# Four of the 22 channel blocks of an up-projection as seven products of halves

## The chip, the cores and the metric

The kernel runs on one core of one Trainium2 chip. The metric is the device time of one execution in microseconds (us). The engines are named as in the profile: PE is the matrix engine, PEld its weight loads, DVE the vector engine, ACT the scalar engine, POOL the third elementwise engine, SP the engine that issues most of the DMA transfers.

## The reference, cut to what matters

The reference is one layer of an encoder on 512 tokens of 1024 channels in float32: a norm, an input projection, two token mixers, a merge, and then a channel mixer. The change touches only the channel mixer:

```
h  = rmsnorm(x)                             # 512 x 1024
u  = h @ w_up                               # 512 x 5632: 2816 gate columns, then 2816 value columns
u  = depthwise conv of width 3 along tokens, centred, with a bias
y  = silu(u[:, :2816]) * u[:, 2816:]        # 512 x 2816
x  = x + y @ w_down                         # 512 x 1024
```

The 2816 channels are 22 blocks of 128. A block needs a gate product and a value product, each of 128 channels by 512 tokens over 1024 inputs.

## The kernel before

Every float32 factor is split into a high and a low part, both in the matrix engine's own float format, and a product is the sum of three: high by high, high by low, low by high. `mm3` issues those three matmuls (L390, L391, L392).

A planner (class `Planner`, L38) collects tasks with an engine, an estimated cost, a key, the names that they read and write, and rings of buffers. It lists them in order of time under its own costs, and the result is one fixed order of instructions for each engine. The engines then run their own orders, and wait on each other through counting semaphores that the framework sets wherever two instructions touch the same tile. A low key means early: FEED (weights) before EVICT (emptying PSUM) before CHAIN (L300).

One up-projection product is one job (`up_job`, L1877; `job`, L433). `weights` (L400) loads 128 columns of `w_up` (512 KB, tile `wr_up`, ring "raw" of three buffers), ACT casts the high half (L413, tile `wh_up`, ring "whi" of two), and POOL subtracts for the low half in two instructions of 128x512 (L421, tile `wl_up`, ring "wlo" of two). Then come 24 matmuls of 128x512 (eight groups of 128 inputs, three each) into one PSUM bank `ps_up` of ring "pp", which has three banks. The token side is `h2` in two parts, shared by all 44 jobs. The first three jobs work on halves of 256 tokens, since `h2` gets ready late.

The bank is emptied by `conv3` (L1943): ACT writes the centre tap with the bias into a tile `c3` (L1948), DVE adds the two outer taps from PSUM (L1954). After a gate and its value, ACT takes the silu (L1976), DVE multiplies (L1974) into `a_0` or `a_1` (blocks 0 to 10 and 11 to 21), and `combine` (L1917) and `split_part` (ACT L1904, DVE L1908) make operands for the down-projection, which already works by seven products of halves (ORDER, TO, L1894). Its weights are prepared in `t_unit` (L1923): two loads of `w_down` rows, four subtractions on POOL (L1939, tile `tp`, ring "tp" of one) and four stores to a scratch tensor; one such unit runs with every second block.

Two other rings matter below: "oo", one tile of two PSUM banks that no job of the up-projection uses, and "dhl", three buffers of 512 KB.

Of the kernel before, what the change touches and what calls it, by code (L numbers as in the profile page):

```python
# [14 lines left out]
P = 128  # L15
S = 512
# [212 lines left out]
def hybrid_block(  # L229
# [1693 lines left out]
    def t_unit(i, u):  # L1923

        b = {}

        def load(r):
            if "w" not in b:
                b["w"] = pools["fp"].tile([P, 2, D], F32, tag="tp", bufs=RINGS["tp"], name=f"tp_{i}")
            k = i + HK * r  # L1930
            sp.dma_start(b["w"][:, r, :], ffn_down[0][k * P : (k + 1) * P, :])

        w = lambda r, c: b["w"][:, r, N_H[c]]
        n = lambda r, c: f"tp:{i}#{r}{c}"
        for r in range(2):
            L(512, lambda r=r: load(r), r=["pool:fp"], w=[n(r, 0), n(r, 1)], key=u, after=() if i else ["pp:up0_1"])

        for j, o, x, y in ((0, (0, 0), (0, 1), (0, 0)), (2, (0, 1), (1, 1), (0, 1)), (1, (1, 1), (1, 1), (0, 0)), (3, (1, 0), (1, 0), (1, 1))):
            G(cp(512), lambda o=o, x=x, y=y: pool.tensor_tensor(out=w(*o), in0=w(*x), in1=w(*y), op=ALU.subtract),  # L1939
              r=[n(*x), n(*y)], w=[n(*o)], key=u)  # L1940
            L(256, lambda j=j, o=o: sp.dma_start(t_scr[j, i], w(*o)), r=[n(*o)], w=[f"ts{j}#{i}"], key=u)

    def conv3(box, pp, ci, b, j, u):  # L1943
        yn = f"cv3:{ci}"

        def centre():
            b[j] = pools["fp"].tile([P, S], F32, tag="cv3", bufs=RINGS["cv3"], name=f"c3_{ci}")
            act.activation(b[j], box["ps"], AF.Identity, scale=fw[:, 1, ci : ci + 1], bias=fw[:, 3, ci : ci + 1])  # L1948

        def tap(k):  # L1950
# [5 lines left out]
                in1=y[:, lo:hi], op0=ALU.mult, op1=ALU.add,  # L1956
            )

        A(0.8, centre, r=[pp, "pool:fp", "small"], w=[yn], key=EVICT + u)
        for k in (0, 2):  # L1960
            V(0.78, lambda k=k: tap(k), r=[pp], w=[yn], key=EVICT + u)

    for c in range(NF):
        b = {}
        for j in range(2):
            box, pp, u = first_jobs.get((c, j)) or up_job(c, j)
            conv3(box, pp, j * NF + c, b, j, u)
        g_, v_ = f"cv3:{c}", f"cv3:{NF + c}"

        def mul(c=c, b=b):  # L1970
            r, i = divmod(c, HK)
            if i == 0:
                a_raw[r] = pools["fp"].tile([P, HK, S], F32, name=f"a_{r}")
            dve.tensor_tensor(out=a_raw[r][:, i, :], in0=b[0], in1=b[1], op=ALU.mult)  # L1974

        A(ca(512), lambda b=b: act.activation(b[0], b[0], AF.Silu), w=[g_], key=u, tab="silu")  # L1976
        V(cd(512), mul, r=[g_, v_], w=[f"ar{c}#0", f"ar{c}#1"], key=u)
        if c < HK:
            split_part(1, c, 1, *blk(c, 0), u + 1)
            s3 = lambda b=b: b[1].rearrange("p (k c) -> p k c", k=2)[:, 0:1]  # L1980
            combine(s3, [v_], blk(c, 0)[0], blk(c, 1)[0], [f"ar{c}"], ALU.subtract, u + 2)
            split_part(7, c, 1, s3, [v_], u + 3)
        else:
            i = c - HK
            combine(*blk(i, 1), blk(i, 1)[0], blk(c, 1)[0], [f"ar{c}#1"], ALU.add, u + 1)
            combine(*blk(i, 0), blk(i, 1)[0], blk(i, 0)[0], [f"ar{i}#1"], ALU.subtract, u + 2)
        if c % 2 == 0:
            t_unit(c // 2, u + 60)


    KEEP = 8
# [248 lines left out]
```

## Time and profile before

| | |
|---|---|
| median of three runs | 874.38 us (873.37 to 874.95) |
| profiled execution, its own time | 874.77 us |
| its span | 873.1 us |
| granted TensorE clock | 0.998 |
| PE busy | 865.3 us, 99% of the span |
| DVE, POOL, ACT busy | 595.0, 532.4, 475.6 us |
| first and last matmul of the up-projection | 518.2 and 760.3 us after the span's start |

The span is the time from the first to the last recorded instruction; the 1.7 us between span and time lie around it. A row of the timeline gives start, duration, engine, line, operation, output and inputs, shapes, and in brackets how long the engine sat idle before it and what ended that. Matmuls are pipelined: the spacing of their starts is their cost, and the duration of one (0.39 us for 128x512) overlaps the next ones.

### The profile page before, as it was taken

What the parts mean: (1) busy time and instruction counts of PE and PEld (TensorE: products, weight loads), DVE (VectorE), ACT (ScalarE), POOL (GpSimd) and SP (SyncE); (2) the same over time, 40 slices, a digit from 0 to 9 for tenths busy, and PEclk for the clock granted to TensorE, in tenths of its full rate; (3) what the DMA queues carried; (4) which work ended last, traced back from release to release, by engine and by line L of the source; (5) the groups of instructions that cost most, each with busy time, mean ns of one, the idle gap of its engine ahead of it and who ended that gap; (6) DMA issues with size and microseconds to landing.
All of it is one profiled execution on the core that took longest, in us unless ns stands there. A gap on an engine that the chain in (4) does not pass through costs nothing.

```text
span 873.1 us, 13883 instructions
## 1 busy us (share of the span) xinstructions
PE 865.3 (99%) x5049; PEld 731.6 (84%) x5049; DVE 595.0 (68%) x1035; ACT 475.6 (54%) x807; POOL 532.4 (61%) x461
## 2 busy tenths in 40 slices
PE   9999999999999999999999999999999999999997
PEld 8888888888888887889888889888888888888886
DVE  5756597357569886555676984656654555579996
ACT  6688554336858634345866665444443333555664
POOL 4445554324546655244597994778777887567763
PEclk9999999999999999999999999999999999999999
DMA  7365447304245463224898005666567666365554
GB/s 210 99 206 134 122 122 165 113 26 133 74 119 157 124 149 93 68 73 134 306 315 281 1 26 155 218 205 209 199 212 237 216 199 198 134 209 181 183 170 151
DMA packets 165512, 138.09 MB, mean 158 GB/s; under 512 B 23662, under 2 KB 133051, under 8 KB 165444
## 3 DMA queue, kind: packets, MB, share of 16 engines
q1 hardware_dynamic: 160706, 135.62, 50.5%
q10 hardware_dynamic: 4738, 1.58, 0.8%
q8 instruction: 40, 0.66, 0.3%
q14 instruction: 28, 0.23, 0.1%
HBM read 113.03 MB, written 24.15 MB: 157 GB/s over the span
## 4 chain that ended last, share of the span: by engine, by line
PE 87%; DVE 6%; POOL 3%; issue 2%; ACT 1%; DMA 1%; POOLq 0%; SPq 0%; DVEq 0%; ACTq 0%
PE ps_up L392 9%; PE ps_up L391 9%; PE ps_up L390 9%; DVE as L1908 2%; PE ps_k L390 2%; PE ps_gd L390 2%; PE ps_k L392 2%; PE ps_gp L390 2%; PE ps_k L391 2%; PE pw L1192 2%; PE ps_gp L392 2%; PE ps_q L392 2%; PE ps_gp L391 2%; PE ps_q L390 2%; PE ps_q L391 2%
## 5 line engine op out<-in xcount | busy, mean ns | idle before, releaser
L421 POOL TENSOR_TENSOR wl_up<-wr_up,wh_up 128x512 fp32r<-128x512 f32 x86 | 111.9, 1322 | 51.8 <-ACT wh_up L413 51.7
L390 PE MATMUL ps_up<-h_hi,wh_up 128*128 128x512 f32 (+1 forms) x360 | 136.8, 380 | 0.0
L392 PE MATMUL ps_up<-h_hi,wl_up 128*128 128x512 f32 (+1 forms) x360 | 136.7, 380 | 0.1
L391 PE MATMUL ps_up<-h_lo,wh_up 128*128 128x512 f32 (+1 forms) x360 | 136.7, 380 | 0.0
L1954 DVE SCALAR_TENSOR_TENSOR c<-ps_up,fw,c 128x511 f32<-128x511 f32 x88 | 66.0, 750 | 99.2 <-ACT c L1948 97.5
L2142 POOL TENSOR_TENSOR w_dn<-wr_dn,w_dn 128x512 fp32r<-128x512 f32 x44 | 65.9, 1513 | 30.9 <-ACT w_dn L2139 27.1
L390 PEld LDWEIGHTS ps_up<-h_hi,wh_up 128*128 128x128 f32 x360 | 67.7, 188 | 12.9
L391 PEld LDWEIGHTS ps_up<-h_lo,wh_up 128*128 128x128 f32 x360 | 67.7, 188 | 12.9
L392 PEld LDWEIGHTS ps_up<-h_hi,wl_up 128*128 128x128 f32 x360 | 67.7, 188 | 12.9 <-POOL wl_up L421 0.3
L413 ACT CAST wh_up<-wr_up 128x1024 fp32r<-128x1024 f32 x43 | 45.2, 1052 | 58.1 <-issue 26.0
L1939 POOL TENSOR_TENSOR tp<-tp 128x512 f32<-128x512 f32 x44 | 61.7, 1402 | 11.7 <-DMA tp<-in_ffn_down_dram 8.0
L2139 ACT CAST w_dn<-wr_dn 128x512 fp32r<-128x512 f32 x69 | 42.2, 621 | 28.6 <-PE dn L392 17.1
L391 PE MATMUL dn<-w_dn,as 128*128 128x512 f32 x141 | 54.3, 385 | 0.0
L390 PE MATMUL dn<-w_dn,as 128*128 128x512 f32 x141 | 54.2, 385 | 0.0
L392 PE MATMUL dn<-w_dn,as 128*128 128x512 f32 x141 | 54.2, 385 | 0.0
L1908 DVE TENSOR_TENSOR as<-a,as 128x512 fp32r<-128x512 f32 (+1 forms) x41 | 41.3, 1032 | 0.1
L1904 ACT CAST as<-a 128x512 fp32r<-128x512 f32 (+1 forms) x41 | 21.5, 535 | 35.0 <-DVE a L1974 30.1
L421 POOL TENSOR_TENSOR wl_k<-wr_k,wh_k 128x512 fp32r<-128x512 f32 x16 | 20.3, 1288 | 28.6 <-ACT wh_k L413 25.6
L1948 ACT ACTIVATE c<-ps_up,fw 128x512 f32<-128x512 f32 x44 | 33.9, 769 | 4.9 <-PE ps_up L392 4.9
L421 POOL TENSOR_TENSOR wl_gp<-wr_gp,wh_gp 128x512 fp32r<-128x512 f32 x16 | 22.3, 1417 | 22.2 <-ACT wh_gp L413 22.2
L421 POOL TENSOR_TENSOR wl_v<-wr_v,wh_v 128x512 fp32r<-128x512 f32 x16 | 21.2, 1347 | 22.7 <-ACT wh_v L413 22.7
L421 POOL TENSOR_TENSOR wl_z<-wr_z,wh_z 128x512 fp32r<-128x512 f32 x16 | 20.4, 1295 | 19.8 <-ACT wh_z L413 19.8
(410 smaller groups left out, 2538.0 us busy)
## 6 DMA issues: line engine op xcount, KB each, us to landing
wr_up<-in_ffn_up_dram SPq DMA_DIRECT2D x44, 512.0 KB, 3.9
tp<-in_ffn_down_dram SPq DMA_DIRECT2D x22, 512.0 KB, 5.2
t_scr<-tp SPq DMA_DIRECT2D x44, 256.0 KB, 2.9
wr_dn<-t_scr SPq DMA_DIRECT2D x20, 512.0 KB, 4.0
wr_dn<-in_ffn_down_dram SPq DMA_DIRECT2D x15, 512.0 KB, 3.7
x<-in_x_dram SPq DMA_DIRECT2D x8, 512.0 KB, 6.4
wr_k<-in_w_in_dram SPq DMA_DIRECT2D x8, 512.0 KB, 4.8
wr_z<-in_w_in_dram SPq DMA_DIRECT2D x8, 512.0 KB, 3.9
```

Of the source, the lines that this page charges most:

```text
L390: pe.matmul(ps, ahi, bhi, start=first, stop=False)
L391: pe.matmul(ps, ahi, blo, start=False, stop=False)
L392: pe.matmul(ps, alo, bhi, start=False, stop=last)
L413: act.copy(b["hi"], b["raw"])
L421: pool.tensor_tensor(out=b["lo"][:, sl], in0=b["raw"][:, sl], in1=f32(b["hi"][:, sl]), op=ALU.subtract)
L1904: act.copy(sets[p][:, i : i + n, 0, :], src())
L1908: dve.tensor_tensor(out=w[:, :, 1, :], in0=src(), in1=f32(w[:, :, 0, :]), op=ALU.subtract)
L1939: G(cp(512), lambda o=o, x=x, y=y: pool.tensor_tensor(out=w(*o), in0=w(*x), in1=w(*y), op=ALU.subtract), r=[n(*x), n(*y)], w=[n(*o)], key=u)
L1948: act.activation(b[j], box["ps"], AF.Identity, scale=fw[:, 1, ci : ci + 1], bias=fw[:, 3, ci : ci + 1])
L1954: dve.scalar_tensor_tensor(out=y[:, lo:hi], in0=box["ps"][:, lo + sh : hi + sh], scalar=fw[:, k, ci : ci + 1], in1=y[:, lo:hi], op0=ALU.mu ...
L2139: act.copy(b["w"][:, 0, :], raw["t"][:, j, :])
L2142: eng.tensor_tensor(out=b["w"][:, 1, :], in0=raw["t"][:, j, :], in1=f32(b["w"][:, 0, :]), op=ALU.subtract)
```

## The change

For channel blocks 4, 6, 8 and 10, `seven_job` takes the place of the gate job and the value job. The 2x2 matrix of weight halves (gate and value rows by first and second 512 inputs) times the 2x2 matrix of token halves (first and second 512 inputs by first and second 256 tokens) is computed as seven products of sums of halves. One product has four input groups of three matmuls of 128x256: 84 such matmuls in place of 48 of 128x512.

- All seven products of a block go into one tile of two PSUM banks, `ps_w` (ring "oo"), with gate in one bank and value in the other, and a half of the tokens in each half of a bank. Product 1 goes to value/first half, 2 to gate/first, 6 to value/first again, 5 to gate/second, 7 to value/second, 4 to value/first, 3 to gate/second.
- Between the products, partial results move: `keep(0)` copies product 1 out to SBUF and `keep(1)` copies a later sum (both ACT, 128x256, L2145). `add_first` adds the first kept piece to both banks in place (DVE, 2x256, L2154), `add_mid` adds the second kept piece to both second halves into an SBUF tile (L2157), `add_end` and `add_last` add those back into PSUM (L2163, L2160). Then `conv3` works on the two banks as before.
- Weights: each block has three sums on POOL and one on DVE (L1986, 128x512), seven casts of 128x512 on ACT (L2081), and seven subtractions for the low parts, four on POOL and three on DVE (L2086), instead of two casts of 128x1024 and four POOL subtractions.
- Tokens: `token_forms`, once, makes four sums of token halves in two parts: 12 instructions of 128x1024 on DVE (nine) and POOL (three) and four casts on ACT. Its buffers are `a_0` for work, one buffer of ring "as", and the place of `a_1`, so the first product into `a_1` (block 11) waits until they are read.
- Moved: one `combine` and the split for product 7 of the down-projection go from blocks 0 to 10 to blocks 11 to 21. The 11 `t_unit`s run with blocks 0, 2, 5, 8, 11 and 12 to 17 instead of every second block, and units 5, 7 and 9 use two "dhl" buffers instead of "tp".

The first place where the order changes is PE at the start of block 6. In the names, `ps_up6_0` is the gate's bank of block 6, `ps_w6` the new two-bank tile, `w_up6f2` the weights of its product 2. Before:

```order
L390 MATMUL ps_up5_1_5905<-h2_hi_5201,wh_up5_1_5864 128x512
L391 MATMUL ps_up5_1_5905<-h2_lo_5202,wh_up5_1_5864 128x512
L392 MATMUL ps_up5_1_5905<-h2_hi_5201,wl_up5_1_5865 128x512
L390 MATMUL ps_up6_0_5945<-h2_hi_5201,wh_up6_0_5909 128x512 [waits DVE_49,Activation_49]
L391 MATMUL ps_up6_0_5945<-h2_lo_5202,wh_up6_0_5909 128x512
L392 MATMUL ps_up6_0_5945<-h2_hi_5201,wl_up6_0_5910 128x512 [waits Pool_49]
```

Each job waits when it starts, for the bank and the two weight parts, and its other matmuls follow. Now, from the last matmul of product 1 on:

```order
L392 MATMUL ps_w6_6002<-h2_hi_5201,w_up6f1_5958 128x256
L390 MATMUL ps_w6_6002<-h2_hi_5201,w_up6f2_5963 128x256 [waits Activation_49]
L391 MATMUL ps_w6_6002<-h2_lo_5202,w_up6f2_5963 128x256
L392 MATMUL ps_w6_6002<-h2_hi_5201,w_up6f2_5963 128x256 [waits DVE_49]
L390 MATMUL ps_w6_6002<-h2_hi_5201,w_up6f2_5963 128x256 [waits Activation_49]
L391 MATMUL ps_w6_6002<-h2_lo_5202,w_up6f2_5963 128x256
```

Product 2 goes to a different bank than product 1, and yet its fourth matmul waits for ACT: the count that it waits for is the one that `keep(0)` raises. The same stands in all four blocks (in block 4 `keep(0)` stands three matmuls later). In the same way, the fourth matmul of product 5 waits for `add_first`, the first of product 7 for `keep(1)`, the seventh of product 4 for `add_mid`, and the first of product 3 for `add_end`. Before the first of product 3 stand three matmuls of 128x512 of the next block's gate; nothing stands between the others and what they wait for. No matmul of the kernel before waits for an access to the tile that it is itself in the middle of filling.

The second place is ACT around the two copies of block 6 (`c3_6` is the block's gate tile, `wh_up7_0` the next gate's high weights, `c3_27` the value tile of block 5):

```order
L2081 CAST w_up6f4_6016<-wr_up6_1_5877 128x512 [waits PE_49]
L2145 COPY c3_6_6025<-ps_w6_6002 128x256 [waits PE_49]
L1962 ACTIVATE c3_27_6031<-ps_up5_1_5953,fw_128 128x512
L2200 ACTIVATE c3_5_5980<-c3_5_5980 128x512 [waits DVE_49,Activation_49]
L413 CAST wh_up7_0_6050<-wr_up7_0_5934 128x1024 [waits DMAHW1_49]
L2145 COPY c3_6_6025<-ps_w6_6002 128x256 [waits DVE_49,PE_49]
```

The first copy waits for PE, and the count is that of product 2's third matmul, not of product 1's last. The second copy waits for DVE (`add_first`) and for PE (the last matmul of product 5).

The third place is DVE, in the same block (`c3_28` is the value tile of block 6, `as_1` an operand of the down-projection):

```order
L1968 SCALAR_TENSOR_TENSOR c3_27_6031<-ps_up5_1_5953,fw_128,c3_27_6031 128x511 [waits DVE_49]
L2154 TENSOR_TENSOR ps_w6_6002<-ps_w6_6002,c3_6_6025 128x2x256 [waits PE_49]
L2198 TENSOR_TENSOR a_0_5498<-c3_5_5980,c3_27_6031 128x512 [waits DVE_49,Activation_49]
L1913 TENSOR_TENSOR as_1_5672<-a_0_5498,as_1_5672 128x256 [waits Activation_49]
L2157 TENSOR_TENSOR c3_28_6102<-ps_w6_6002,c3_6_6025 128x512 [waits PE_49]
L2163 TENSOR_TENSOR ps_w6_6002<-ps_w6_6002,c3_28_6102 128x256 [waits DVE_49,PE_49]
L2160 TENSOR_TENSOR ps_w6_6002<-ps_w6_6002,c3_28_6102 128x2x256 [waits DVE_49,PE_49]
L1968 SCALAR_TENSOR_TENSOR c3_6_6025<-ps_w6_6002,fw_128,c3_6_6025 128x511 [waits DVE_49,Activation_49]
```

`add_first` waits for the third matmul of product 5, `add_mid` for the sixth of product 4, `add_end` for the twelfth of product 4, `add_last` for the end of product 3. Between two of them stand the product and the split of block 5.

The diff, cut to its core:

```diff
+    SEVEN = (4, 6, 8, 10)
+    FORMS = (1, 2, 6, 5, 7, 4, 3)
+    LO_ENG = dict(zip(FORMS, "GVGVGVG"))
+    SUM_ENG = "GVGG"
+    TOK_ENG = "VGVVVVVGVVGV"
...
+    def seven_job(c, b):
...
+        for j in range(2):
+            L(512, lambda j=j: load(j), w=[f"{rn[j]}#0", f"{rn[j]}#1"], key=feed + j)
...
+        total(s1, a21, a22, ALU.add, 2)
+        total(s2, s1, a11, ALU.subtract, 3)
+        for k, (f, src) in enumerate(((1, a11), (2, a12), (6, s2), (5, s1))):
+            wn[f] = form(f, src, k)
+        total(a21, a11, a21, ALU.subtract, 14)
+        total(a12, a12, s2, ALU.subtract, 15)
+        for k, (f, src) in enumerate(((7, a21), (4, a22), (3, a12))):
+            wn[f] = form(f, src, k + 4)
...
+        where = {1: (1, 0), 2: (0, 0), 6: (1, 0), 5: (0, 1), 7: (1, 1), 4: (1, 0), 3: (0, 1)}
...
+        def spot(a, i):
+            if "t" not in ps:
+                ps["t"] = banks2(f"ps_w{c}")
+            return ps["t"][:, a, 256 * i : 256 * i + 256]
...
+        def mm(f, k):
+            w = wt_[f]
+            sl = slice(k * P, (k + 1) * P)
+            mm3(spot(*where[f]), w[:, 0, sl], w[:, 1, sl], *right(f, k), k == 0, k == 3)
...
+        def product(f):
+            for k in range(4):
+                M(0.361, lambda k=k: mm(f, k), r=[wn[f], *rname(f, k)], w=[on(*where[f]), f"turn{c}"], key=u + 10 * turn["n"] + k)
+            turn["n"] += 1
...
+        def keep(i):
+            A(ca(256), lambda: act.copy(pieces(0)[:, i, :], spot(1, 0)), r=[on(1, 0), "pool:fp"], w=[pn[i]], key=top)
...
+        def add_first():
+            dve.tensor_tensor(out=both(0), in0=both(0), in1=twice(pieces(0)[:, 0:1, :]), op=ALU.add)
+
+        def add_mid():
+            dve.tensor_tensor(out=pieces(1), in0=both(1), in1=twice(pieces(0)[:, 1:2, :]), op=ALU.add)
+
+        def add_last():
+            dve.tensor_tensor(out=both(1), in0=both(1), in1=twice(pieces(1)[:, 0:1, :]), op=ALU.add)
+
+        def add_end():
+            dve.tensor_tensor(out=spot(1, 0), in0=spot(1, 0), in1=pieces(1)[:, 1, :], op=ALU.add)
+
+        product(1)
+        keep(0)
+        product(2)
+        product(6)
+        V(cd(512), add_first, r=[pn[0]], w=[on(0, 0), on(1, 0)], key=top)
+        keep(1)
+        product(5)
+        product(7)
+        V(cd(512), add_mid, r=[on(0, 1), on(1, 1), pn[1], "pool:fp"], w=[pn[2], pn[3]], key=top)
+        product(4)
+        product(3)
+        V(cd(512), add_last, r=[pn[2]], w=[on(0, 1), on(1, 1)], key=top)
+        V(cd(256), add_end, r=[pn[3]], w=[on(1, 0)], key=top)
...
+    APART = (5, 7, 9)
+    UNITS = (0, 2, 5, 8, 11, 12, 13, 14, 15, 16, 17)
```

More of the change, by code (lines that the diff above doesn't have):

```diff
@@ L1899, in hybrid_block, with a_half @@
     sets = {}
+    def a_half(r):
+        if a_raw[r] is None:
+            a_raw[r] = pools["fp"].tile([P, HK, S], F32, tag=f"a{r}", name=f"a_{r}")
+        return a_raw[r]
     def part_hi(p, i, n, src):
@@ L1925, in t_unit @@
         b = {}
+        apart = i in APART
         def load(r):
-            if "w" not in b:
-                b["w"] = pools["fp"].tile([P, 2, D], F32, tag="tp", bufs=RINGS["tp"], name=f"tp_{i}")
+            if apart:
+                b[r] = pools["fp"].tile([P, D], F32, tag="dhl", bufs=RINGS["dhl"], name=f"tp_{i}{r}")
+            elif not r:
+                t = pools["fp"].tile([P, 2, D], F32, tag="tp", bufs=RINGS["tp"], name=f"tp_{i}")
+                b[0], b[1] = t[:, 0, :], t[:, 1, :]
             k = i + HK * r
-            sp.dma_start(b["w"][:, r, :], ffn_down[0][k * P : (k + 1) * P, :])
-        w = lambda r, c: b["w"][:, r, N_H[c]]
-        n = lambda r, c: f"tp:{i}#{r}{c}"
+            sp.dma_start(b[r], ffn_down[0][k * P : (k + 1) * P, :])
+        w = lambda r, c: b[r][:, N_H[c]]
+        n = lambda r, c: f"dhl:t{i}{r}#{c}" if apart else f"tp:{i}#{r}{c}"
         for r in range(2):
@@ L1941, in t_unit, with conv3 @@
             L(256, lambda j=j, o=o: sp.dma_start(t_scr[j, i], w(*o)), r=[n(*o)], w=[f"ts{j}#{i}"], key=u)
-    def conv3(box, pp, ci, b, j, u):
+    def conv3(box, pp, ci, b, j, u, late=None):
         yn = f"cv3:{ci}"
+        pp = pp if late else [pp]
         def centre():
-            b[j] = pools["fp"].tile([P, S], F32, tag="cv3", bufs=RINGS["cv3"], name=f"c3_{ci}")
+            if late:
+                box["ps"] = late()
+            if j not in b:
+                b[j] = pools["fp"].tile([P, S], F32, tag="cv3", bufs=RINGS["cv3"], name=f"c3_{ci}")
             act.activation(b[j], box["ps"], AF.Identity, scale=fw[:, 1, ci : ci + 1], bias=fw[:, 3, ci : ci + 1])
@@ L1957, in tap @@
             )
-        A(0.8, centre, r=[pp, "pool:fp", "small"], w=[yn], key=EVICT + u)
+        A(0.8, centre, r=[*pp, "pool:fp", "small"], w=[yn], key=EVICT + u)
         for k in (0, 2):
-            V(0.78, lambda k=k: tap(k), r=[pp], w=[yn], key=EVICT + u)
+            V(0.78, lambda k=k: tap(k), r=pp, w=[yn], key=EVICT + u)
+    SEVEN = (4, 6, 8, 10)
[3 more added lines that the diff above has]
+    TOK_ENG = "VGVVVVVGVVGV"
+    forms = {}
@@ L1963, in hybrid_block @@
+    APART = (5, 7, 9)
+    UNITS = (0, 2, 5, 8, 11, 12, 13, 14, 15, 16, 17)
     for c in range(NF):
         b = {}
-        for j in range(2):
+        if not c:
+            token_forms()
+        if c in SEVEN:
+            u = seven_job(c, b)
+        for j in range(2 if c not in SEVEN else 0):
             box, pp, u = first_jobs.get((c, j)) or up_job(c, j)
```

127 lines of the change are left out of this document (118 added, 9 removed).

## The prediction

> **What bounds the kernel now.** The page's busy times come first, then the chain that ended last, then busy time by stretches of the up-projection.
>
> ```profile
> span 873.1 us, 13883 instructions
> PE 865.3 (99%) x5049; PEld 731.6 (84%) x5049; DVE 595.0 (68%) x1035; ACT 475.6 (54%) x807; POOL 532.4 (61%) x461
> ...
> PE 87%; DVE 6%; POOL 3%; issue 2%; ACT 1%; DMA 1%; POOLq 0%; SPq 0%; DVEq 0%; ACTq 0%
> ```
>
> ```profile
> core 0: us, PE busy (x) PEld busy (x) DVE busy (x) ACT busy (x) POOL busy (x), PEclk, DMA share, GB/s
> 530.00:568.00 38.00, 38.00 (x200) 32.75 (x199) 21.38 (x28) 18.47 (x26) 24.60 (x19) 1.00 0.53 175
> 560.00:600.00 40.00, 40.00 (x178) 33.14 (x177) 21.50 (x29) 18.11 (x26) 30.77 (x24) 1.00 0.67 214
> 600.00:640.00 40.00, 40.00 (x179) 33.10 (x178) 24.87 (x31) 17.57 (x26) 31.30 (x24) 1.00 0.67 224
> 640.00:680.00 40.00, 40.00 (x178) 33.14 (x177) 22.20 (x27) 15.72 (x21) 31.37 (x25) 1.00 0.64 204
> 720.00:765.00 45.00, 45.00 (x200) 37.28 (x199) 25.69 (x33) 19.56 (x28) 29.10 (x23) 1.00 0.50 166
> ```
>
> In every stretch PE is busy for all of it, at full granted clock. So a microsecond of matmul taken out is a microsecond gained, and a microsecond in which PE stands still is one lost, since there is no idle time of PE to absorb it. POOL comes next (31 of 40), then DVE and ACT at about half.
>
> **What is removed: matmul time.** The spacing of the starts tells it. First and last row of two dense stretches of the timeline:
>
> ```profile
> 546.37 0.39 PE L390 MATMUL ps_up<-h_hi,wh_up 128*128 128x512 f32 x1
> ...
> 551.80 0.39 PE L390 MATMUL ps_up<-h_hi,wh_up 128*128 128x512 f32 x1
> ```
>
> ```profile
> 531.74 0.28 PE L390 MATMUL ps_up<-h_hi,wh_up 128*128 128x256 f32 x1
> ...
> 537.50 0.40 PE L390 MATMUL ps_up<-h_hi,wh_up 128*128 128x512 f32 x1
> ```
>
> 24 matmuls of 128x512 lie between the first pair: 5.43/24 = 0.226 us each. 48 of 128x256 lie between the second: 5.76/48 = 0.120. A block cost 48 x 0.226 = 10.86 and will cost 84 x 0.120 = 10.08 of matmul time. That is 0.78 less, and 3.1 us for four blocks: an eighth of 10.86 would be 1.36, and the rest of it goes into the fixed part of the shorter matmuls.
>
> The Trainium skill ("TensorE: Matmul & The Clock Gate", "Back-to-back issue gap") gives N/2.4 + 2.5 ns for an isolated matmul at full clock, so by estimate 215.8 and 109.2 ns, and 1.19 us less for a block, 4.7 in all. The rows have 226 and 120, a fixed part of 14 ns, and they decide; by the page the sum below would end 1.6 us earlier.
>
> **What is added: waits in the middle of a block.** A job of the kernel before waits when it starts, for a bank that was emptied long ago. In the changed order PE waits five times inside a block for an ACT or DVE instruction on the tile that it is filling, and each of these in turn waits for the very matmul before (product 3, below, apart). ACT and DVE cannot come early, so PE pays for the whole way there and back. No row before has such a round trip whole, but its pieces are there:
>
> ```profile
> 531.62 0.28 PE L392 MATMUL ps_up<-h_hi,wlo_up 128*128 128x256 f32 x1
> 532.07 0.78 ACT L1948 ACTIVATE c<-ps_up,fw 128x512 f32<-128x512 f32 x1 [4.88 <-PE ps_up L392]
> 532.88 0.75 DVE L1954 SCALAR_TENSOR_TENSOR c<-ps_up,fw,c 128x511 f32<-128x511 f32 x1 [4.97 <-ACT c L1948]
> ...
> 866.45 0.28 PE L392 MATMUL dn<-wt_lo,as 128*128 128x256 f32 x1
> 866.77 0.42 DVE L2018 TENSOR_TENSOR x<-dn,x 128x256 f32<-128x256 f32 x1 [0.56 <-PE dn L392]
> ```
>
> ```profile
> 521.22 0.28 PE L391 MATMUL ps_up<-h_lo,wh_up 128*128 128x256 f32 x1
> 521.56 0.19 PEld L392 LDWEIGHTS ps_up<-h_hi,wl_up 128*128 128x128 f32 x1 [0.27 <-POOL wl_up L421]
> 521.56 0.39 PE L392 MATMUL ps_up<-h_hi,wl_up 128*128 128x256 f32 x1
> 521.78 0.28 PE L390 MATMUL ps_up<-h_hi,wh_up 128*128 128x256 f32 x1
> ```
>
> ```profile
> L1593 ACT CAST ms<-ps_do x8: 348/372/374, 443.5 to 483.4; 128x256 fp32r<-128x256 f32 x8
> ...
> L1580 DVE TENSOR_TENSOR ps_do<-ps_do,gdl x8: 686/700/700, 441.8 to 477.9; 128x512 f32<-128x512 f32 x8
> ```
>
> - From the start of a matmul of 128x256 to the start of a reader that stood waiting for it: 0.45 (531.62 to 532.07), 0.32 (866.45 to 866.77). Behind the second PE ran dry, as it will here, so I take 0.35.
> - From the end of one engine's instruction to the start of the other that waits: 532.07 + 0.78 = 532.85 to 532.88, 0.03.
> - After a stall the next spacing is 0.22 (521.56 to 521.78), not 0.12: the weight load lies open, 0.10 more. If the weights can be loaded before the wait, it is 0.
> - The access: an ACT copy of 128x256 out of PSUM 0.37, an in-place DVE addition of 128x512 in PSUM 0.70.
>
> A `keep` costs PE 0.35 + 0.37 + 0.03 + 0.10, less the 0.12 that the spacing takes anyway: 0.73 (0.60 with nothing for the weights and 0.32 ahead, 0.83 with 0.45). `add_first` and `add_mid` cost 0.33 more each: 1.06 (0.93 to 1.16). `add_end` (128x256, 0.42 as at 866.77) takes 0.35 + 0.42 + 0.03 = 0.80, and PE has three matmuls of the next gate for it, 0.12 + 3 x 0.226 = 0.80: 0 (to 0.20). `add_last` has nobody on PE waiting for some 10 us. One block: 2 x 0.73 + 2 x 1.06 = 3.58 (3.06 to 4.18); four: 14.3 (12.2 to 16.7).
>
> Whether the waiting engine is free when its matmul is done: ahead of `keep(0)` stands the cast for product 4, which waits for the end of the previous job, 15 matmuls (1.8 us) earlier, and takes some 0.6. Between the two copies stand a centre tap (0.78), a silu and a cast of 128x1024, some 2.5 us together, and PE needs about 5 between them. Ahead of `add_first` stand two taps (0.75 each) that end 2.3 us after `keep(0)`, where PE needs over 3 for the rest of product 2, product 6 and three matmuls. So 0, with 0.5 per block (2 in all) as the upper end. Behind `keep(0)` on ACT are the centre tap of the block before and the cast of the next gate's weights; both are used a product or more later.
>
> **What is added on POOL, DVE and ACT.** Durations, from the groups of the page:
>
> ```profile
> L421 POOL TENSOR_TENSOR wl_up<-wr_up,wh_up 128x512 fp32r<-128x512 f32 x86 | 111.9, 1322 | 51.8 <-ACT wh_up L413 51.7
> ...
> L1954 DVE SCALAR_TENSOR_TENSOR c<-ps_up,fw,c 128x511 f32<-128x511 f32 x88 | 66.0, 750 | 99.2 <-ACT c L1948 97.5
> ...
> L390 PEld LDWEIGHTS ps_up<-h_hi,wh_up 128*128 128x128 f32 x360 | 67.7, 188 | 12.9
> ...
> L1939 POOL TENSOR_TENSOR tp<-tp 128x512 f32<-128x512 f32 x44 | 61.7, 1402 | 11.7 <-DMA tp<-in_ffn_down_dram 8.0
> ```
>
> In a pair of blocks, one of the new kind and one of the old, POOL has three sums and eight low parts at 1.32 and four subtractions of a `t_unit` at 1.40: 20.1 us. PE needs 10.1 + 10.9 = 21.0 without the waits, and 24.5 with them. POOL stays under it because the waits stretch the pair; without them its cover would be 0.9 us. I cost it at 0. The token sums and splits (12 of 128x1024, of which POOL has three, each some 2 x 1.32 = 2.6) fall between 530 and 568, where POOL has 13 us free and DVE 17: 0; a POOL sum that comes just ahead of weights that PE needs would cost up to 2.6. The moved `combine` and split (one of each in blocks 11 to 21) add some 1.5 us of DVE to 10.9 us of a block, where DVE has 4 or 5 free, and the moved units send the same number of transfers through SP's queue, where the weight loads of the gates and values stand behind them; these are fetched a job or more ahead: 0.
>
> **The sum.** 874.77 (the profiled execution) - 3.1 + 14.3 = 886.0. That execution lies 0.4 above the median of 874.38, so 885.6 for a median. From its bounds: -3.1 + 12.2 gives 883.5, -3.1 + 16.7 + 2 gives 890.
>
> **The rivals.**
>
> (A) *The waits cost next to nothing.* The place is the same four waits; the point is 0.78 us a block, under 0.2 us for each. That holds if ACT and DVE are released when the matmul is issued and PE's queue covers the access. The time is 874.4 - 3.1 = 871.3, faster than before. For it: PE hardly stood still anywhere in the rows of before. Against it: no matmul there had to wait for an access to its own tile, and the access alone (0.37, 0.70) is longer than 0.2. Chance 0.05.
>
> (B) *Half of it is hidden*: the waits come to 0.6 to 1.0 us a block, because releases overlap with the drain of matmuls in flight. That is -0.7 to +0.9, about 874.5. Against it stand the 0.32 and 0.45 of the rows. Chance 0.04.
>
> (C) *POOL becomes the bound.* In the trace single subtractions take up to 1.75 (the first two low parts of 128x512 by L1869 among them):
>
> ```profile
> 524.42 1.74 POOL L1869 TENSOR_TENSOR wlo_up<-wr_up,whi_up 128x512 fp32r<-128x512 f32 x1
> ```
>
> The change gives DVE eight more instructions per block, four of them with both inputs in SBUF like POOL's. If these made every POOL instruction as long as this row, a pair would take 15 x 1.74 = 26.1, against 24.5 with the waits: 1.6 more each, 6.4 in all, 892. Against it: the means, 1.32 and 1.40, in a stretch with DVE busy for half the time. Chance 0.07.
>
> (D) *Weight loads set the spacing.* A load takes 0.188 whatever the width of the matmul, and there are 84 instead of 48: 84 x 0.188 = 15.8, 4.9 more than a block now, 19.7 in all, about 894 without any wait. The rows of 128x256 speak against it: 48 loads in 5.76 us overlap two deep. Chance 0.03. The same section of the Trainium skill leans this way: for a stream of pairs of load and matmul it states about 81 ns at width 128 and 131 at 512, by estimate 98 at 256, so that 84 shorter ones would take 1.9 us more than 48 long ones. The rows' 120 and 226 do not bear that out.
>
> **How the numbers follow.** The forecast has 0.81: 885.6, with its own range 883 to 890. (A) 0.05, (B) 0.04, (C) 0.07, (D) 0.03. To hold 8 in 10 the range takes in the bounds and a little on both sides: 881 (waits a fifth shorter than the lowest bound) to 891.5 (up to where C begins). A measurement of this kernel tells some 0.2%, 1.75 us, from no change. Slower by more than that: forecast, C and D, 0.91; faster: A, 0.05; the same: B, 0.04.
>
> **What would show it.** In the changed kernel's trace, PE idles inside `ps_w`, four times a block, released by ACT L2145 twice, and by DVE L2154 and L2157, with spacings of 0.8 to 0.9 and 1.1 to 1.3 us; PE's idle time over the up-projection is 12 to 17 us; the matmuls of 128x256 stand 0.12 apart elsewhere. After block 10 PE is dense again and the rest takes as long as now. POOL ends its low parts before PE asks for them. I am wrong if the gaps are missing or much shorter (A, B), if PE waits for POOL in blocks 4 to 11 (C), or if the dense spacing in `ps_w` is over 0.13 (D). I would also be wrong if the moved units held up blocks 11 to 17.

## The result and the profile after

| | before | changed | ratio |
|---|---|---|---|
| median | 874.66 us | 898.22 us (896.30 to 900.63) | 1.027 [1.025, 1.029] |
| profiled execution | 874.77 us | 896.30 us | |
| its span, granted clock | 873.1 us, 0.998 | 894.6 us, 0.996 | |

The direction was as forecast, the size was not: 23.6 us slower, where 11 were forecast, and 6.7 above the range. The page of the changed kernel has these lines on busy times and on the chain that ended last:

```profile
span 894.6 us, 14267 instructions
PE 868.7 (97%) x5193; PEld 737.5 (82%) x5193; DVE 655.1 (73%) x1076; ACT 487.9 (55%) x839; POOL 570.6 (64%) x476
...
PE 24%; DVE 12%; POOL 2%; ACT 2%; issue 1%; DMA 1%; DVEq 0%; ACTq 0%; POOLq 0%
```

The chain is followed back only to 519 us here, so the shares add up to 42%; in these 376 us alone DVE has twice the 6% of the span that it had in the whole chain before. PE's busy time rose by 3.4 us, though there is less to multiply: around a stall a matmul is recorded as 0.39 or 0.42 where it was 0.28 (rows below), so only the spacing of the starts tells what one costs. The stretches of the up-projection, in the columns shown before:

```profile
core 0: us, PE busy (x) PEld busy (x) DVE busy (x) ACT busy (x) POOL busy (x), PEclk, DMA share, GB/s
530.00:568.00 38.00, 36.24 (x193) 30.92 (x192) 35.68 (x27) 19.02 (x25) 34.07 (x18) 1.00 0.36 113
568.00:610.00 42.00, 32.76 (x200) 28.85 (x199) 30.50 (x33) 18.55 (x32) 33.75 (x24) 0.96 0.46 146
610.00:640.00 30.00, 26.82 (x160) 23.17 (x159) 19.82 (x23) 12.59 (x21) 25.73 (x19) 1.00 0.47 152
640.00:680.00 40.00, 36.82 (x198) 31.41 (x197) 29.65 (x33) 17.39 (x28) 34.49 (x26) 1.00 0.77 252
```

Two things stand out. PE has 1.8 to 9.2 us of idle time in each. And in 530 to 568, where the token sums run, DVE is busy for 35.7 of 38 us (21.4 before) and POOL for 34.1 (24.6 before): both are nearly full. The waits of PE, grouped (total, number, longest):

```profile
PE ps_w L390 <- ACT c L2145: 7.1, 8, 3.3
PE ps_w L390 <- DVE ps_w L2154: 4.7, 4, 1.3
PE ps_w L390 <- DVE c L2157: 3.2, 4, 0.9
PE ps_up L392 <- POOL wl_up L421: 1.5, 2, 1.2
...
PE ps_w L392 <- DVE w_up4f L2086: 0.6, 1, 0.6
PE ps_w L392 <- POOL w_up4f L2086: 0.5, 1, 0.5
```

Sixteen of these are the four forecast waits in four blocks: 15.0 us. One of them is 3.3 us long and not 0.6. It is the first copy of block 4, on PE's timeline:

```profile
570.05 0.28 PE L392 MATMUL ps_w<-h_hi,w_up4f 128*128 128x256 f32 x1
573.66 0.39 PE L390 MATMUL ps_w<-h_hi,w_up4f 128*128 128x256 f32 x1 [3.33 <-ACT c L2145]
573.88 0.37 PE L391 MATMUL ps_w<-h_lo,w_up4f 128*128 128x256 f32 x1
574.05 0.42 PE L392 MATMUL ps_w<-h_hi,w_up4f 128*128 128x256 f32 x1
574.26 0.42 PE L390 MATMUL ps_w<-h_hi,w_up4f 128*128 128x256 f32 x1
```

DVE's and ACT's rows of the same time show why that copy came late:

```profile
569.46 0.68 DVE L1986 TENSOR_TENSOR s<-s,wr_up 128x512 f32<-128x512 f32 x1
```

```profile
570.17 1.14 ACT L2081 CAST w_up4f<-s 128x512 fp32r<-128x512 f32 x2 [1.90 <-DVE s L1986]
571.68 0.63 ACT L2200 ACTIVATE c<-c 128x512 f32<-128x512 f32 x1 [0.37 <-DVE c L1968]
572.22 1.12 ACT L2081 CAST w_up4f<-wr_up 128x512 fp32r<-128x512 f32 x2
573.24 0.36 ACT L2145 COPY c<-ps_w 128x256 f32<-128x256 f32 x1
```

DVE, which in its timeline has no idle time from 551.8 to 575.8, comes to a weight sum of block 4 only at 569.46. Four casts and a silu stand ahead of the copy on ACT, and they wait for that sum and for two taps of DVE.

After the stop PE's matmuls stand 0.21 apart and not 0.12, for 17 of them, and a window over this piece shows a granted clock of 0.58 where all stretches before had 1.00:

```profile
574.00:578.00 4.00, 3.93 (x21) 3.73 (x19) 1.78 (x2) 2.25 (x3) 4.00 (x3) 0.58 0.20 56
```

So the profiled run's 21.5 us fall into these pieces (each is the spacing of two starts less the spacing that they take anyway):

| piece | us |
|---|---|
| matmul time saved, four blocks | -3.1 |
| four waits in blocks 6, 8 and 10, and the open weight load behind each, 3 x 4.2 | 12.6 |
| the same and two late weights in block 4 | 8.1 |
| half pace behind block 4's long wait, 17 x 0.093 | 1.6 |
| weights from POOL late at 554 | 1.5 |
| weights from POOL late at 722 and 728 | 0.9 |
| sum | 21.6 |

The other executions have a granted clock of 0.990 to 0.994 and are up to 4.3 us longer than the profiled one; the median lies 1.9 above it.

### The profile page after: what moved, and what is told of

It reads as the page before. It is cut to its first block, busy times and chain, and to the rows that moved or that the text cites. A ratio compares the mean times of both kernels' runs of the same rounds, so it can differ in the third digit from the quotient of the medians.

```text
span 894.6 us, 14267 instructions
## 1 busy us (share of the span) xinstructions
PE 868.7 (97%) x5193; PEld 737.5 (82%) x5193; DVE 655.1 (73%) x1076; ACT 487.9 (55%) x839; POOL 570.6 (64%) x476
## 3 DMA queue, kind: packets, MB, share of 16 engines
q10 hardware_dynamic: 4738, 1.58, 0.8%
## 5 line engine op out<-in xcount | busy, mean ns | idle before, releaser
L421 POOL TENSOR_TENSOR wl_up<-wr_up,wh_up 128x512 fp32r<-128x512 f32 x70 | 99.4, 1439 | 29.7 <-ACT wh_up L413 22.6
L392 PE MATMUL ps_up<-h_hi,wl_up 128*128 128x512 f32 (+1 forms) x296 | 112.3, 379 | 1.6 <-POOL wl_up L421 1.5
L390 PE MATMUL ps_up<-h_hi,wh_up 128*128 128x512 f32 (+1 forms) x296 | 112.1, 379 | 0.0
L391 PE MATMUL ps_up<-h_lo,wh_up 128*128 128x512 f32 (+1 forms) x296 | 111.9, 378 | 0.0
L1968 DVE SCALAR_TENSOR_TENSOR c<-ps_up,fw,c 128x511 f32<-128x511 f32 x72 | 53.8, 747 | 31.2 <-ACT c L1962 29.9
L392 PEld LDWEIGHTS ps_up<-h_hi,wl_up 128*128 128x128 f32 x296 | 55.7, 188 | 13.6 <-POOL wl_up L421 3.1
L391 PEld LDWEIGHTS ps_up<-h_lo,wh_up 128*128 128x128 f32 x296 | 55.7, 188 | 10.1
L390 PEld LDWEIGHTS ps_up<-h_hi,wh_up 128*128 128x128 f32 x296 | 55.7, 188 | 9.9
L2200 ACT ACTIVATE c<-c 128x512 f32<-128x512 f32 x22 | 13.9, 631 | 34.2 <-DVE c L1968 34.2
L421 POOL TENSOR_TENSOR wl_gd<-wr_gd,wh_gd 128x512 fp32r<-128x512 f32 x16 | 20.7, 1314 | 18.3 <-ACT wh_gd L413 18.3
```

Source lines behind the costliest of these rows:

```text
L390: pe.matmul(ps, ahi, bhi, start=first, stop=False)
L391: pe.matmul(ps, ahi, blo, start=False, stop=False)
L392: pe.matmul(ps, alo, bhi, start=False, stop=last)
L421: pool.tensor_tensor(out=b["lo"][:, sl], in0=b["raw"][:, sl], in1=f32(b["hi"][:, sl]), op=ALU.subtract)
L1968: dve.scalar_tensor_tensor(out=y[:, lo:hi], in0=box["ps"][:, lo + sh : hi + sh], scalar=fw[:, k, ci : ci + 1], in1=y[:, lo:hi], op0=ALU.mu ...
```

## The experiments

The theory to test had two halves: the waits on the tile cost about 3.5 us a block, and the rest, some 9 us, comes from the token sums, which make DVE and POOL late. Rivals: that the waits themselves are the whole of it, that late instructions come from the moved units, and that POOL is simply short of time.

**Without the token sums (no_tokens).** Products 4 to 7 take plain halves of the tokens instead of sums; all else stays.

```diff
-            return [forms[f]["t"][i][:, k, :] for i in range(2)]
+            q = Q_OF[f]
+            return [h2[i][:, 4 * q[0] + k, 256 * q[1] : 256 * q[1] + 256] for i in range(2)]
...
-        if not c:
-            token_forms()
```

> The token sums and their splits are left out; products 4 to 7 take plain halves of the tokens instead, so sums of token halves are missing from the result. If the stage in which the token sums run (12 instructions of 128x1024 between 532 and 562 us) makes the weights late, the gap of 1.4 us at 554 goes, those of 0.69, 0.71 and 2.9 of the 3.49 us in block 4 go too, and with them the slow clock behind the long one (1.7 us): 7 to 8 us less than 898.2, 890 to 891.5. Blocks 6, 8 and 10 keep their 4.2 us each. If the weights of block 4 are late by themselves (eleven sums and low parts more on POOL and DVE), its gaps stay and the time is over 895.

Measured: 888.49 us, 1.016 [1.014, 1.017], 9.7 under the changed kernel and 1.5 below what I expected. The stop at 554, the long wait in block 4 and the half pace are gone. The four waits of blocks 4, 6 and 8 are now alike in each: 0.62, 0.95, 0.62, 0.94, and 0.10 behind each, 3.53 us a block. `keep(0)` and `add_first` of block 6 on the timeline, with the matmuls on both sides:

```profile
591.20 0.28 PE L392 MATMUL ps_w<-h_hi,w_up6f 128*128 128x256 f32 x1
591.52 0.37 ACT L2148 COPY c<-ps_w 128x256 f32<-128x256 f32 x1 [0.67 <-PE ps_w L392]
591.94 0.39 PE L390 MATMUL ps_w<-h_hi,w_up6f 128*128 128x256 f32 x1 [0.46 <-ACT c L2148]
...
594.80 0.28 PE L392 MATMUL ps_w<-h_hi,w_up6f 128*128 128x256 f32 x1
595.12 0.70 DVE L2157 TENSOR_TENSOR ps_w<-ps_w,c 128x512 f32<-128x512 f32 x1 [0.52 <-PE ps_w L392]
595.87 0.39 PE L390 MATMUL ps_w<-h_hi,w_up6f 128*128 128x256 f32 x1 [0.79 <-DVE ps_w L2157]
```

(The line numbers have moved by three.) 0.32 from the matmul's start to the reader, the access, and 0.05 back to PE. With the -3.1 of matmul time the four blocks alone account for 11.0 of the 14.1 us by which this kernel is slower than before; most of the rest are waits of PE for POOL at 707 to 726 (0.57, 0.33 and 1.34) and one longer `add_first` in block 10 (0.63).

**Only the token sums (tokens_only), and neither (moved_only).** No block by seven products. The first still makes the sums, which nobody reads; the second leaves them out too, so that only the moved `combine`s and `t_unit`s remain of the change.

```diff
-    SEVEN = (4, 6, 8, 10)
+    SEVEN = ()
```

> No block by seven products; the token sums are still made (and not used), and the moved work stays moved. By the theory of waits and late weights: the gap at 554 (1.4 us with its weight load) and the two near 725 (0.9) remain, 2 to 3 us over 874.7: 876.5 to 878. If the moved units and splits or the token sums are a larger part, 880 or more.

> No block by seven products and no token sums: only the moved units and the moved combine and split are left of the change. With the token sums this stood at 880.8. If the token sums carry those 6.4 us, 874 to 875.5, no change; if the moves carry a part of it, 876 or more, with waits of PE for low parts in blocks 11 to 17.

Measured: 880.81 us, 1.007 [1.005, 1.009], with the sums, 2.8 above what I expected, and 873.03 us, 0.9986 [0.9976, 0.9995], without. What I had moved past the queues costs nothing. The sums cost 7.8 us, though PE reads nothing of them. Counted from 873.03, the sums alone add 7.8, the four blocks alone (888.49) 15.5, and both together (898.22) 25.2: only 1.9 more than the two added up. So most of what the sums cost does not need a block by seven products. PE's waits in the first of the two are five of one kind:

```profile
PE ps_up L392 <- POOL wl_up L421: 4.2, 5, 1.2
```

**The sums on DVE alone (tok_v), and then with one input in PSUM (tok_psum).** Both build on tokens_only. The first puts POOL's three of the 12 instructions on DVE. The second is the first, except that each of the 12 reads one of its two inputs from a PSUM tile, filled once by ACT. Number, size and engine stay; the unused sums are of other numbers.

```diff
-    TOK_ENG = "VGVVVVVGVVGV"
+    TOK_ENG = "VVVVVVVVVVVV"
...
-            fused(next(eng), 1024, xs(q), part(0, q), part(1, q), ALU.add, names + ["pool:fp"], xn(q), key)
+            fused(next(eng), 1024, xs(q), dv, part(1, q), ALU.add, ["oo:dum"] + names + ["pool:fp"], xn(q), key)
```

> As the run with the token sums alone (880.8), but all 12 instructions of the sums and splits go to DVE, none to POOL. The theory is that DVE instructions with both inputs in SBUF and POOL instructions lock each other out: 12 x 1.22 us of DVE then still hold POOL off in a stretch where POOL has 13 us free of 38, and low parts stay late: 876 to 881, with POOL's L421 near 1.7 us in that stretch. If it was only the three sums in POOL's own queue, the waits go: 873 to 874.5.

> The same 12 DVE instructions in the same places and shapes, but the first input is a tile of two PSUM banks that ACT has filled once (the values of the sums are not those of the tokens, and nothing uses them). By the lock, DVE no longer holds POOL off: L421 at 1.29 us, no waits of PE near 547 to 592, and the time of the run without token sums, 873 to 874.5. If DVE's time or its order (taps behind the sums) is the cause, it is as slow as the run before it.

Measured: 886.30 us, 1.013 [1.011, 1.015], and 877.02 us, 1.003 [1.002, 1.004]. To take POOL's part off POOL made it worse, which I had not expected; where one operand lies makes 9.3 us. The window and two groups (count, shortest/median/longest in ns, when), first of tok_v:

```profile
530.00:568.00 38.00, 33.77 (x163) 27.94 (x162) 35.46 (x26) 17.88 (x22) 32.42 (x18) 0.91 0.60 201
```

```profile
L1986 DVE TENSOR_TENSOR a<-a x4: 2143/2242/2311, 542.7 to 557.1; 128x1024 f32<-128x1024 f32 x4
L421 POOL TENSOR_TENSOR wl_up<-wr_up,wh_up x20: 1279/1304/2286, 535.4 to 596.5; 128x512 fp32r<-128x512 f32 x20
```

and of tok_psum:

```profile
530.00:568.00 38.00, 38.00 (x200) 32.77 (x200) 31.70 (x32) 20.16 (x26) 31.71 (x25) 1.00 0.79 256
```

```profile
L1986 DVE TENSOR_TENSOR a<-dum,a x4: 1214/1215/1216, 541.7 to 551.8; 128x1024 f32<-128x1024 f32 x4
L421 POOL TENSOR_TENSOR wl_up<-wr_up,wh_up x23: 1259/1297/1747, 536.0 to 599.5; 128x512 fp32r<-128x512 f32 x23
```

With both inputs in SBUF an instruction of 128x1024 takes 2.24 us, with one in PSUM 1.22. That is also what the first of the changed kernel takes, which starts 0.04 us ahead of one of the same size on POOL; those after it take twice as long:

```profile
532.11 1.22 DVE L1986 TENSOR_TENSOR a<-h_hi,h_lo 128x1024 f32<-128x1024 f32 x1 [4.09 <-PE ps_up L392]
...
538.04 2.13 DVE L1986 TENSOR_TENSOR a<-h_hi,h_lo 128x1024 f32<-128x1024 f32 x1
540.10 2.32 DVE L1986 TENSOR_TENSOR a<-a 128x1024 f32<-128x1024 f32 x1
```

A low part on POOL takes 1.30, and up to 2.29 beside such instructions. So a DVE instruction with two inputs in SBUF and a POOL instruction hold each other off, and the recorded durations contain the standing by. The Trainium skill ("SBUF — State Buffer", "Who interferes with whom") states this: a DVE instruction with both inputs in SBUF and a GpSimd instruction that reads SBUF contend for a port pair that is an exclusive lock, and one with at most one input there (outside the engine's two-port modes) does not. Trace and page agree, and the rows give its price here: 1.0 us for a DVE instruction, up to 1.0 for one of POOL.

The time of tok_psum is 2.5 us above what I expected. What tok_psum still loses are two stops of 0.97 and 1.80, for a low part of POOL; at the second, POOL stood behind a subtraction of a `t_unit` that waited for its load:

```profile
593.16 1.28 POOL L1949 TENSOR_TENSOR tp<-tp 128x512 f32<-128x512 f32 x1 [2.71 <-DMA tp<-in_ffn_down_dram]
```

**The changed kernel with its sums made so (seven_tok_psum).** The same edit on the whole change, so the sums are of other numbers.

> The changed kernel with its four blocks, and the 12 token sums and splits all on DVE with the first input in PSUM (their values are not those of the tokens, so the products 4 to 7 are not either). If the 9.7 us of the token stage are the mutual lock of DVE and POOL, and the slow clock that follows from it, they go although DVE does the same number of sums: 888 to 891, the time of the run without token sums, with block 4 at the gaps of the plain waits (0.62, 0.95, 0.62, 0.94). If DVE's time is what counts, block 4 stays late and the time is over 895.

Measured: 899.26 us, 1.029 [1.027, 1.031]: 8 us above what I expected, in the range of the rival, and no faster than the changed kernel. The stop at 554 is gone, and PE now stands still for 7.5 us at block 4. This is why (ACT and DVE, timeline):

```profile
572.21 3.21 DVE L2207 TENSOR_TENSOR a<-c,c 128x512 f32<-128x512 f32 x2
```

```profile
573.83 0.37 ACT L2154 COPY c<-ps_w 128x256 f32<-128x256 f32 x1 [3.75 <-DVE a L2207]
```

The first copy of block 4 writes into a buffer of the ring "cv3", which has four. It needs the one that the multiplication of an earlier block frees, and that stood in DVE's order behind low parts, taps and splits. Before the change the gate's `c3` buffer was wanted when the gate's 24 matmuls were done, 5.4 us after the block's start; `keep(0)` wants it after 12 short ones, 1.4 us. The lock between the sums and POOL is not the only source of lateness, then: what else stands in DVE's order in front of block 4 is another. Part of that is the lock again, on the weights' instructions: a sum of 128x512 at 559.8 takes 0.69 us on DVE there, and the low parts of block 4 take 1.58 to 1.78.

**Three blocks instead of four (no4).** The first block by seven products comes two blocks later, with more time behind the token sums.

```diff
-    SEVEN = (4, 6, 8, 10)
+    SEVEN = (6, 8, 10)
```

> Seven products in blocks 6, 8 and 10 only; the first stands some 22 us later behind the token sums. If the late weights belong to the token stage and not to the block, PE still waits for low parts between 547 and 592 as in the run with the token sums alone (880.8), and three blocks add 3.5 to 4.2 - 0.8 us each: 889 to 891.5. If they belong to the first block by seven products itself, it is late again at 590, with a gap of over 2 us: 895 or more.

Measured: 889.62 us, 1.018 [1.016, 1.019], in the first range. But the sign of the other reading, a gap of over 2 us near 590, is there too: the stops of block 6, now the first, are 0.76, 2.28, 0.95, 0.62 and 0.94, and `add_first` of blocks 8 and 10 costs 1.49 and 1.45 instead of 0.95. So lateness goes with the first block by seven products, wherever it is, but not without the sums: in no_tokens the first block has the four plain waits and nothing more. I could not separate the two further.

**One name for the whole tile (tile_names).** The planner believes that the four parts of `ps_w` are separate. Here it is told the truth of the semaphores, one name for the tile, so that it may put other work between a product and what waits for its tile.

```diff
-        on = lambda a, i: f"{o}#{a}{i}"
+        on = lambda a, i: o
```

> Only the names that the planner is given change: all pieces of the two-bank tile get one name, as the framework sees them. The planner then puts nine matmuls of the next gate ahead of product 4, and product 2 waits for the first copy when it starts, product 5 for the second copy (and through it for the first addition). By the prices measured: 0.72 + 1.42 us a block instead of 4.2, 8 us less in all: 889 to 891. If the waits are not the cause, no change from 898.

Measured: 902.25 us, 1.032 [1.030, 1.033]: a miss of over 11 us, and slower than the changed kernel. The planner did move matmuls of the next gate ahead of product 4, and now these wait for weights of POOL that come late:

```profile
PE ps_w L390 <- ACT c L2145: 11.4, 5, 4.9
PE ps_up L392 <- POOL wl_up L421: 8.9, 7, 2.8
```

At 601 the second copy came 3 us late, because it stood on ACT behind a split's cast that waited for DVE:

```profile
603.99 0.41 ACT L1909 CAST as<-a 128x256 fp32r<-128x256 f32 x1 [3.44 <-DVE a L2198]
```

Four of its stops are longer than 2.8 us, and the granted clock of 568 to 680 is 0.88 to 0.96.

**A tile for each bank (two_tiles).** Gate and value get a tile each, the two-bank additions become two, and products run in the order 1, 2, 6, 5, 7, 3, 4, so that a whole product lies between every access and the next matmul that has to wait for it.

```diff
-                ps["t"] = banks2(f"ps_w{c}")
-            return ps["t"][:, a, 256 * i : 256 * i + 256]
+                ps[a] = bank("ds", f"ps_w{'gv'[a]}{c}")
+            return ps[a][:, 256 * i : 256 * i + 256]
...
+        add_first(0)
+        add_first(1)
+        add_mid(0)
+        add_mid(1)
```

> The two banks of a block become two tiles, each addition over both banks becomes two of one bank, and products 3 and 4 change places, so that between any product and the ACT or DVE instruction it waits for stands one whole product of the other bank (1.44 us). If the waits on the own tile are the cause, PE's gaps inside blocks 6, 8 and 10 (0.80, 1.45, 0.62 and 0.94 us, with 0.10 behind each: 4.2 a block) go, and 3 of the 7 us in block 4: some 15.5 us less than 898.2, 881 to 884. The late weights of block 4 and the slow clock behind them stay. If instead POOL and DVE are the bound and the waits only hide it, PE then waits for low parts (POOL, DVE L2086) in all four blocks, and the time stays at 890 or more.

Measured: 891.71 us, 1.019 [1.018, 1.021], in the range of the rival. Of the four waits of block 6 one late one of 0.82 is left. The four waits had cost some 14 us over the four blocks, yet only 6.5 us came back. The waits view shows what took their place:

```profile
PE ps_wv L390 <- ACT c L2144: 5.7, 5, 2.6
PE ps_up L392 <- POOL wl_up L421: 4.7, 7, 1.2
PE ps_wv L392 <- POOL w_up8f L2086: 1.3, 1, 1.3
```

Once PE does not stop, POOL is what it waits for. A low part `wl_up` between 568 and 665 takes 1.51 on the mean here (1.32 before, 1.36 in the changed kernel). Single low parts and copies are late in blocks 8 and 10, and block 4 has its long copy as ever (2.78).

**The same with weight sums and low parts on DVE (tt_dve), without token sums (tt_no_tokens, plain halves as in no_tokens), and without the subtractions of the `t_unit`s as well (tt_no_tokens_no_tp).** The last leaves 44 instructions out of the down-projection's weights.

```diff
-    LO_ENG = dict(zip(FORMS, "GVGVGVG"))
-    SUM_ENG = "GVGG"
+    LO_ENG = dict(zip(FORMS, "VVVVVVV"))
+    SUM_ENG = "VVVV"
```

> Two tiles a block, token sums made; all four weight sums and all seven low parts of a block go to DVE (before: seven of these eleven on POOL). A DVE instruction of this kind takes 0.68 us alone and a POOL one 1.29, and both lock each other out. If the bound in these blocks is the time in which either holds the port, the waits for weights in blocks 6 to 10 (some 8 us in the run with two tiles) shrink by half or more: 884 to 888. If DVE becomes the bound, as its own additions and taps then stand behind the low parts, 892 or more.

> Two tiles a block and no token sums (products 4 to 7 take plain halves of the tokens; the sums are missing from the result). If the token sums cost what they cost with one tile (9.7 us) and nothing takes their place, 891.7 - 9.7 = 882. Of that 874.4 - 3.1 = 871.3 is matmul time, and the other 8 to 11 us would be waits for low parts of weights on POOL in blocks 6 to 17. If the late weights come from the token stage only, they go too, and the time is 872 to 874.

> As the run before, and the four POOL subtractions of each t_unit are left out too, so the weights of the down-projection are stored as they were loaded: 44 instructions of 1.4 us less on POOL. If POOL's work is what PE still waits for, the waits for low parts go and the gain in matmul time stands: 871 to 873, faster than before. If it is the loads of raw weights and their three buffers, most of the waits stay: over 877.

| | median | ratio | what PE still waits for |
|---|---|---|---|
| two_tiles | 891.71 | 1.019 [1.018, 1.021] | POOL, late copies, half pace |
| tt_dve | 893.69 | 1.022 [1.020, 1.024] | POOL's `wl_up` (5.5 us in five waits), DVE (2.5 and 1.9) and ACT; DVE is busy for 36.3 of 42 us at 568 to 610, clock 0.92 there |
| tt_no_tokens | 879.86 | 1.007 [1.004, 1.010] | POOL: 39.5 of 40 us busy at 640 to 680 |
| tt_no_tokens_no_tp | 874.73 | 1.000 [0.999, 1.001] | four stops, 0.81, 0.36, 0.84 and 1.28 |

The work cannot go from POOL to DVE, which is full too. It has to go away: 11.9 us less without the token sums, 5.1 less again without the subtractions. The last kernel has no wait for `wl_up`. Three of its four stops are still waits for a copy or an addition on the bank, one in block 6, 8 and 10 each, that comes late, and one (0.84) is for a low part; together (3.3, and 0.1 behind each) they eat the whole saving of 3.1. I had expected 871 to 873.

**A stop of chosen length (stall_short, stall_long).** To price the half pace by itself: the kernel before, with copies on ACT ahead of the high weights of block 8's gate, where PE then waits once. The cast writes the weights behind the copies, so the computation is whole. Four copies of 128x512 for the long stop (shown), one of 128x128 for the short one.

```diff
+        if name == "up8_0":
+            for i in range(4):
+                A(0.01, lambda: act.copy(b["hi"][:, 0:4, :].rearrange("p k c -> p (k c)"), boxes["up7_1"]["ps"][:, 0:512]), r=["pp:up7_1", f"raw:{name}"], w=[whi], key=feed)
+            A(0.01, lambda: act.copy(b["hi"], b["raw"]), r=[f"raw:{name}", "pp:up7_1"], w=[whi], key=feed)
```

> The kernel before, and one wait added: ahead of the gate of block 8, ACT waits for the end of the value of block 7, copies 128x128 out of its bank over the weights and casts the weights again (1.05 us). PE stands still once, for about 0.35 + 0.25 + 1.05 + 0.05: 1.5 to 1.8 us, the granted clock stays at 1.00, and the time is 876 to 876.5.

> As the run before, with four copies of 128x512 instead of one of 128x128: PE stands still once, for 3.5 to 4 us. If a stall of more than about 2 us makes the granted clock fall, the matmuls behind it go at half pace for some 3.4 us and 1.6 us more are lost: 879.5 to 880.5. If the slow stretches in block 4 have another cause, only the stall itself is lost: 878 to 878.5, with the clock at 1.00.

Measured: 876.95 us, 1.002 [1.001, 1.003], and 880.33 us, 1.006 [1.005, 1.008]. The long one's stop:

```profile
607.71 0.39 PE L392 MATMUL ps_up<-h_hi,wl_up 128*128 128x512 f32 x1
...
612.52 0.80 PE L390 MATMUL ps_up<-h_hi,wh_up 128*128 128x512 f32 x1 [4.42 <-ACT wh_up L434]
613.11 0.63 PE L391 MATMUL ps_up<-h_lo,wh_up 128*128 128x512 f32 x1
```

It lost 4.6 us by standing still and 2.6 behind: the second matmul came 0.59 after the first, and the next eleven stood 0.427 apart (0.226 at full clock). From the first matmul of the up-projection to its last it took 249.3 us, and 242.1 before; about 1 us of that came back in the stages around it. The short stop came out at 2.4 us, longer than meant, because a cast stood ahead of the copies; against my expectation it too was followed by half pace, from 0.6 us later on for 3.4 us, and cost 1.6 more. Not every time, it seems: two of its executions have a granted clock of 0.999 and take 875.6 us, the profiled one 0.997 and 878.27.

## Why the prediction was right and wrong

- *A microsecond of PE standing still is one lost.* Right: the pieces of the profiled run come to 21.6 of 21.5 us.
- *Removed, 3.1 us.* Right: matmuls of 128x256 stand 0.120 apart in `ps_w` wherever nothing holds them.
- *Four waits, 3.58 us a block, of them 0.10 each for an open weight load.* Right: 3.53 in no_tokens, each of the four within 0.02 of its term. Rivals A and B fall with it.
- *`add_end` at 0.* Right: at product 3 there is no wait, only an open weight load of 0.10.
- *"So 0, with 0.5 per block (2 in all) as the upper end"* for a waiting engine that is not free. Mis-sized: 0.7 in each of blocks 6, 8 and 10, and 3.0 in block 4, where two late weights add 1.6. In block 6, `add_first` came 0.50 late: DVE still had a low part of 1.79 and two taps ahead of it. In block 4, `keep(0)` came late because ACT's casts ahead of it waited for a weight sum of DVE. I had looked at what stands between two of the waits, not at how far behind the engine already was.
- *"The token sums and splits ... fall between 530 and 568, where POOL has 13 us free and DVE 17: 0".* Wrong, and the main failure: without them the change is 9.7 us faster, and they alone cost the kernel before 7.8 more than the moved work does. The free times were read for each engine apart. But the nine on DVE hold POOL off while they run, and are held off by it, so they take from both: by the rows' prices 9 x 1.22 and 3 x 2.6, an estimate of 18.8 us, would have had to fit where POOL had 13 free, and in that stretch DVE had 35.7 of 38 us and POOL 34.1. Shown by an edit is the lock for the kernel without blocks by seven products (tok_v against tok_psum); in the changed kernel the same edit brought nothing back (seven_tok_psum), so how the 9.7 divide between the lock of the sums and the rest of DVE's order is open. I had even given C such a mechanism, for the weights' instructions; for the sums, which are twice as wide, I had not asked it.
- *The clock.* The sum has no term for it. It is 1.6 us in the profiled run and, by their lower granted clock, probably more in the others.
- *POOL at 0, "without them its cover would be 0.9 us".* Nearly right, apart from the stretch of the sums: PE waited 0.9 us for POOL after block 10, and 0.7 for one low part in block 4. In two_tiles, where the waits are covered, POOL does become what PE waits for. Rival C had the right pair of engines, and a price from the wrong place: POOL's `wl_up` between 568 and 665 took 1.36 on the mean and not 1.74.
- *The moved units at 0.* Right: 0.9986 [0.9976, 0.9995], at most a gain that lies inside what this kernel's measurement tells.
- *Rival D.* Fell: 84 loads at a spacing of 0.120.

With 3.53 for a block in place of 3.58, the terms that held give 885.8 in the profiled run (874.77 - 3.1 + 14.1). The rest up to 896.3 is lateness (1.5 at 554, 4.6 in block 4, 2.0 in the other blocks, 0.9 after them) and the 1.6 at half pace.

Open is how the sums make blocks 6, 8 and 10 late, 40 to 80 us after them. The weights of the seven products alone do not do it in blocks 4, 6 and 8 (no_tokens has them, and no lateness there; in block 10 it has 0.6). But with each edit the planner also changes the orders of DVE and ACT, so the path from the sums to these blocks is not shown.

None of these versions beats the kernel before by more than the measurement tells; even with the waits covered and two kinds of work left out, the saving of 3.1 us does not show.

## What to carry to other kernels

A wait on the tile that an engine is in the middle of filling costs a whole round trip, and its pieces can be read from rows of a kernel that has no such wait: lag to the reader, access, release, and the weight load that lies open afterwards. Before work goes into an engine's free time, add up what all engines need that hold each other off there, and look where in the orders the engine is already late; free time per engine is not additive. And a small saving on the engine that sets the end is worth only as much as the next engine's slack: here 3 us of matmul time cost POOL and DVE more than they had.

## What the runs showed of the hardware that was not expected

- **A stop of PE can cost again after it, and its length alone does not decide.** Behind some stops a matmul of 128x512 took 0.427 instead of 0.226 and one of 128x256 0.213 instead of 0.120. In each trace the changes of the granted clock lie whole multiples of 3.413 us apart, and in the up-projection the slow stretches last one or two of these; 3.41 us at half pace cost about 1.6 (stall_short, and block 4 of the changed kernel). A stop of 2.06 was followed by half pace (tt_dve), stops of 2.29 (no4) and 2.42 (seven_tok_psum) were not, and in seven_tok_psum half pace followed stops of 1.44 and 0.62. Laid on that raster, the 16 traces agree over the up-projection: in every step of 3.41 us at full pace that was followed by half pace PE stood idle for 1.85 us or more, and in no other such step for more than 1.80 (spacing beyond 0.226 or 0.120, pieces over 0.2 us). The stop of 2.42 lay across a border, 1.25 on one side and 1.17 on the other. Where a stop falls on the raster may also be why stall_short is not slow in every execution; no run shows that. The Trainium skill ("TensorE: Matmul & The Clock Gate", "Part 1: The HAM clock gate (the "warmup" mystery)") has the clock halved after an idle window of about 3.4 us, and full again after about 3.4 us of work. The half pace and the 3.4 us agree; that the whole window has to be idle does not, since 1.85 us within one were enough.
- **Where one operand lies can be worth more than which engine does the work**: 9.3 us between tok_v and tok_psum, with the same 12 instructions in the same order on the same engine; by estimate 4.4 of them are half pace behind tok_v's two longest stops (some 22 matmuls at 0.427 instead of 0.226).
